# Two small tiles move to the right end of SBUF, and the pools of that side shift by 448 bytes

## The chip, the core and the metric

The kernel runs on one core of a Trainium2 chip. The metric is the device time of one execution in microseconds (us); the time of a kernel is the median of its runs. The core has a matrix engine (PE in the profile; PEld is its loading of weights), a vector engine (DVE), a scalar engine (ACT), GpSimd (POOL) and SyncE (SP), which here issues nearly all DMAs. Work is held in SBUF, 128 partitions; an address below is a byte offset within each partition.

## The reference

A trunk of two layers is applied to two groups of tokens, 512 and 256, of width 1,024, in float32 with shared weights. Cut to what matters:

```python
def swiglu(h, wg, wu, wd):
    return (jax.nn.silu(h @ wg) * (h @ wu)) @ wd

def even_layer(x, ...):                     # layer 0
    x = x + 0.5 * swiglu(rmsnorm(x, f1_n), f1_g, f1_u, f1_d)
    x = x + mixer_ab(rmsnorm(x, mix_n), ...)  # gMLP gating and windowed attention
    x = x + 0.5 * swiglu(rmsnorm(x, f2_n), f2_g, f2_u, f2_d)
    return x
# odd_layer (layer 1) is the same with mixer_c, a 2-D neighbourhood attention
# trunk: even_layer, odd_layer, final rmsnorm
```

The hidden width of the feed-forward blocks is 2,816. `rmsnorm(x, g)` multiplies by a scale vector `g`; there are seven of them, one for each of the six blocks and the final one.

## The kernel before

**Stages.** `build` (line 1408) runs six phases in order: `l0f1`, `l0m`, `l0f2`, `l1f1`, `l1m`, `l1f2`, that is, feed-forward, mixer, feed-forward for each layer, and then the final norm. The activations `x` stay in SBUF as 8 tiles of 128 features x 768 tokens, in two halves of 384 tokens.

**A product in float32.** Each operand is split into a high and a low part of type fp32r (`split`, line 193, for activations; `wsplit`, line 103, for weights: ACT copies the high part, DVE subtracts to get the low one). `mm3` (line 175) then issues three matmuls into one PSUM tile: high x high, high x low, low x high. All go through `mmul`, so they have line 139 in the profile. The first operand, weights, is loaded into the array; the second, the *moving* operand, streams through it.

**A feed-forward block.** `ffn` (line 416) works on 11 pairs of hidden tiles (`pair`, line 459), for `gate` and `up`. The product of a pair, 2 x 2 blocks in features, hidden units and tokens, is formed with seven block products in place of eight, from sums and differences of blocks. The combinations of the activations are made once per block: `b11`, `b21`, `t1`, `t2`, `t3`, `n4`, `b22`, each as four tiles of 128 x 384 for the high (`h`) and the low part (`l`). They live in the pool `comb` (`ffn_open`, `ffn_tiles`, lines 303 to 313). The sums of weights (`s`) and everything else of a pair live in the pool `work`: 30 buffers of 128 x 384 for hidden values and their split combinations (`db..`, `dt..`, `dn..`), and 8 of 128 x 512. A block product is 4 steps of 128 features x 3 matmuls of 384 columns. The first four pairs (`EARLY`) are interleaved, as their operands and the norm's scales come one after another. After every second pair `down` (line 628) multiplies the hidden values of two pairs by the down weights, again with seven products; the last two pairs go through `down_last` (line 693).

**Weights.** `raw` (line 91) issues a 512 KB DMA on SP's queue for each block of weights into a rotating pool of four buffers. The parts that `wsplit` makes, `whi` and `wlo`, rotate through five buffers each of the pool `w`.

**Order of the work.** The matmuls are issued in the order in which the program text writes them, with attention and norm steps woven in by a clock of estimated matmul time (`spawn`, `tick`). On the other engines the framework orders instructions by priority and by when their operands are there, and puts in every wait.

**Where tiles lie.** The pools made in `__init__` are allocated at the left end and stay: constants (`const`: identity, ones, the scale vectors `gains` and their negatives `ngains`), `x`, `raw`, `w`, `norm`. What is left between them and the right end of SBUF is shared by the pools of the phases, opened with a side (`open`, line 80), left or right, from which they grow. `comb` and `work` have opposite sides, and so have the mixer's pools `xg` (the split activations, later the split attention output) and `mp` (all else):

| Phase | left | right |
|---|---|---|
| `l0f1` | `work` | `comb` |
| `l0m` | `mp` | `xg` |
| `l0f2`, `l1f1` | `comb` | `work` |
| `l1m` | `xg` | `mp` |
| `l1f2` | `work` | `comb` |

In the built program the left ones begin at address 73,760 and the right ones end at 229,344. Pools are opened with `reuse_waits="tile"`: a tile in memory that an earlier pool has released waits for the last uses of the earlier tiles that it overlaps, not for the whole pool.

Of the kernel before, what the change touches and what calls it, by code (L numbers as in the profile page):

```python
# [9 lines left out]
F32 = mybir.dt.float32  # L10
# [6 lines left out]
P = 128  # L17
D = 1024
KD = D // P
# [9 lines left out]
NORMS = ("l0_ffn1_norm", "l0_mix_norm", "l0_ffn2_norm", "l1_ffn1_norm", "l1_mix_norm", "l1_ffn2_norm", "final_norm")  # L29
# [22 lines left out]
class Trunk:  # L52
# [4 lines left out]
    def __init__(self, ctx, tc, aps, phases=PHASES):  # L57
        self.tc, self.nc, self.aps, self.phases = tc, tc.nc, aps, phases
        self.units = []
        self.woff = self.pi = 0  # L60
        self.t = 0.0
        self.chains = []
        self.spare = []
        self.first = []
        self.copied = []
        pool = lambda name, bufs, **kw: ctx.enter_context(tc.tile_pool(name=name, bufs=bufs, **kw))
        self.cp = pool("const", 1)
        self.xp = pool("x", 1)
        self.rawp = pool("raw", 4)
        self.wp = pool("w", NW)  # L70
        self.np_ = pool("norm", 1)
        self.mm = pool("mm", 4, space=bass.MemoryType.PSUM)
        self.aux = pool("aux", 4, space=bass.MemoryType.PSUM)
        self.dram = pool("spill", 1, space=bass.MemoryType.DRAM)
        self.guards = {}
        self.side = "left"
# [1331 lines left out]
    def build(self):  # L1408
        nc = self.nc
        self.ident = self.cp.tile([P, P], F32, tag="ident", name="ident")  # L1410
        make_identity(nc, self.ident)
        self.ones = self.cp.tile([P, P], F32, tag="ones", name="ones")
        nc.gpsimd.memset(self.ones, 1.0)
        self.onesr = self.cp.tile([P, P], F32R, tag="onesr", name="onesr")
        nc.vector.tensor_copy(self.onesr, self.ones)
        self.gains = self.cp.tile([P, KD * len(NORMS)], F32, tag="gains", name="gains")
        nc.scalar.dma_start(self.gains, self.aps["gains"])
        self.ngains = self.cp.tile([P, KD * len(NORMS)], F32, tag="ngains", name="ngains")
        nc.gpsimd.tensor_scalar(out=self.ngains, in0=self.gains, scalar1=-1.0, scalar2=None, op0=ALU.mult)
        self.x = [self.xp.tile([P, T], F32, tag=f"x{m}", name=f"x{m}") for m in range(KD)]  # L1420
        todo = [KIND[p] for p in self.phases] + [("last", 6)]
        kind = todo[0][0]
        if kind == "f":
            self.ffn_open("right")
            self.ffn_tiles()
            self.fw = self.open("work", "left")
        elif kind != "last":
            self.mixer_tiles("right")
        self.norm_begin(todo[0])
        for h, (c0, c1) in enumerate(HALVES):  # L1430
            for m in range(KD):
                nc.sync.dma_start(self.x[m][:, c0:c1], self.aps["x"][m, :, c0:c1])
                if not (h and kind == "f"):
                    self.final(m, c0, c1)
                if h == 0 and m % 4 == 3 and kind == "f":
                    pre = f"{self.phases[0][:2]}_ffn{self.phases[0][3]}"
                    self.first += [self.raw(f"{pre}_w_{n}", 0, KD, m // 4 * 2 * P, P) for n in ("gate", "up")]
            if h and kind == "f":
                self.spawn(self.second())
            elif kind in ("f", "last"):  # L1440
                self.half_done(h)
            if kind == "last":
                self.drain()
        for i, ph in enumerate(self.phases):
            self.following = todo[i + 1]
            if i == 0 and "l1m" in self.phases:
                self.bias_tables()
            if ph == "l1m":
                while self.spare:
                    self.spare.pop(0)()  # L1450
            if ph == "l0m":
                self.mixer0()
            elif ph == "l1m":
                self.mixer1()
            else:
                self.ffn(f"{ph[:2]}_ffn{ph[3]}")
        self.drain()
        for n in list(self.guards)[::-1]:
            self.close(n)
# [103 lines left out]
```

## Time and profile before

| | |
|---|---|
| median of 3 runs | 2648.54 us |
| the runs | 2646.51, 2648.54, 2650.86 us |
| the profiled execution, first to last instruction | 2646.8 us |
| PE, PEld busy | 2576.9 us (97%), 2505.0 us (95%) |
| DVE, ACT, POOL busy | 2272.7 us (86%), 1369.5 us (52%), 87.9 us (3%) |
| mean granted clock of PE | 0.990 |
| moved by DMA | 218.99 MB, 83 GB/s |

The profile is one execution; it gives its span and no other time of that execution. Busy time is the union of an engine's instructions. Matmuls are pipelined: the duration of one (some 340 ns) is longer than the distance from one to the next, so the pace is read from how many fit in a stretch, or from the chain of waits. That chain is followed back from the last instruction, at each step to what released it or to the instruction before it on its engine; a piece of it in the listing is a run of instructions of one kind, with start, length and count. A row of a window gives, for each engine, busy us and the number of instructions, then the granted clock and the DMA's share and rate.

### The profile page before, as it was taken

What the parts mean: (1) busy time and instruction counts of PE and PEld (TensorE: products, weight loads), DVE (VectorE), ACT (ScalarE), POOL (GpSimd) and SP (SyncE); (2) the same over time, 40 slices, a digit from 0 to 9 for tenths busy, and PEclk for the clock granted to TensorE, in tenths of its full rate; (3) what the DMA queues carried; (4) which work ended last, traced back from release to release, by engine and by line L of the source; (5) the groups of instructions that cost most, each with busy time, mean ns of one, the idle gap of its engine ahead of it and who ended that gap; (6) DMA issues with size and microseconds to landing.
All of it is one profiled execution on the core that took longest, in us unless ns stands there. A gap on an engine that the chain in (4) does not pass through costs nothing.

```text
span 2646.8 us, 41176 instructions
## 1 busy us (share of the span) xinstructions
PE 2576.9 (97%) x15094; PEld 2505.0 (95%) x15094; DVE 2272.7 (86%) x4793; ACT 1369.5 (52%) x2851; POOL 87.9 (3%) x172
## 2 busy tenths in 40 slices
PE   7999999998999999999999999999999999999997
PEld 7999999987899999999999999989898999999997
DVE  8998889889769988898999888886677699988886
ACT  7544444555656544445654544454455465454443
POOL 0000000000100000000000000002222100000000
PEclk9999999999999999999999999999999999999999
DMA  5323222431222222222222221232221332222221
GB/s 173 127 83 91 76 79 66 133 98 37 86 74 100 80 80 65 80 72 88 96 80 80 64 80 65 84 119 65 63 63 40 104 104 80 80 72 72 70 83 56
DMA packets 83898, 218.99 MB, mean 83 GB/s; under 512 B 20080, under 2 KB 32880, under 8 KB 83696
## 3 DMA queue, kind: packets, MB, share of 16 engines
q1 hardware_dynamic: 83552, 216.34, 25.4%
q8 instruction: 118, 1.93, 0.3%
q14 instruction: 84, 0.69, 0.1%
q10 hardware_dynamic: 144, 0.03, 0.0%
HBM read 206.90 MB, written 15.07 MB: 84 GB/s over the span
## 4 chain that ended last, share of the span: by engine, by line
PE 88%; DVE 7%; ACT 2%; DMA 1%; issue 1%; SPq 0%; DVEq 0%; ACTq 0%
PE ps_mm L139 55%; PE ps_aux L139 32%; DVE wlo L114 1%; DMA raw<-in_w 1%; PE ps_aux L143 1%; ACT p L910 1%; DVE xl L738 1%; ACT whi L113 0%; DVE p L919 0%; DVE tl L196 0%; DVE p L904 0%; DVE s L608 0%; ACT xh L737 0%; DVE ol L196 0%; DVE x L705 0%
## 5 line engine op out<-in xcount | busy, mean ns | idle before, releaser
L113 ACT CAST whi<-s 128x512 fp32r<-128x512 f32 x496 | 305.4, 622 | 396.3 <-DVE s L608 142.8
L113 ACT CAST whi<-raw 128x512 fp32r<-128x512 f32 x512 | 312.3, 621 | 265.6 <-PE ps_mm L139 119.5
L114 DVE TENSOR_TENSOR wlo<-s,whi 128x512 fp32r<-128x512 f32 x496 | 338.3, 688 | 71.0 <-ACT whi L113 70.6
L114 DVE TENSOR_TENSOR wlo<-raw,whi 128x512 fp32r<-128x512 f32 x494 | 339.5, 695 | 26.7 <-ACT whi L113 23.8
L139 PE MATMUL ps_aux<-dt,whi 128*128 128x384 f32 x864 | 222.7, 339 | 2.1 <-ACT whi L113 2.1
L139 PE MATMUL ps_mm<-db,whi 128*128 128x384 f32 x864 | 221.6, 338 | 0.0
L139 PEld LDWEIGHTS ps_aux<-dt,whi 128*128 128x128 f32 x864 | 157.6, 189 | 2.4 <-ACT whi L113 2.4
L139 PEld LDWEIGHTS ps_mm<-db,whi 128*128 128x128 f32 x864 | 156.8, 188 | 0.0
L139 PE MATMUL ps_mm<-xh,whi 128*128 128x512 f32 (+1 forms) x416 | 147.5, 355 | 4.0 <-ACT xh L737 4.0
L139 PE MATMUL ps_aux<-dt,wlo 128*128 128x384 f32 x432 | 146.7, 340 | 0.2 <-DVE wlo L114 0.2
L139 PE MATMUL ps_mm<-db,wlo 128*128 128x384 f32 x432 | 146.1, 338 | 0.0
L139 PE MATMUL ps_mm<-xl,whi 128*128 128x512 f32 (+1 forms) x416 | 142.5, 343 | 1.1 <-DVE xl L738 1.1
L139 PE MATMUL ps_mm<-xh,wlo 128*128 128x512 f32 (+1 forms) x416 | 142.2, 342 | 0.0
L498 DVE TENSOR_TENSOR u<-ps_aux,u 128x384 f32<-128x384 f32 x176 | 97.6, 555 | 4.2 <-PE ps_aux L139 3.5
L608 DVE TENSOR_TENSOR s<-raw,raw 128x512 f32<-128x512 f32 x124 | 83.9, 688 | 18.1 <-DMA raw<-in_w 18.1
L139 PE MATMUL ps_aux<-dh,whi 128*128 128x384 f32 x384 | 98.4, 338 | 0.7 <-DVE x L705 0.7
L608 DVE TENSOR_TENSOR s<-raw 128x512 f32<-128x512 f32 x124 | 85.4, 690 | 14.2 <-DMA raw<-in_w 13.7
L910 ACT ACTIVATE p<-p,st 128x256 f32<-128x256 f32 (+3 forms) x144 | 69.1, 483 | 54.8 <-DVE st L908 54.6
L660 DVE TENSOR_TENSOR x<-ps_aux,x 128x384 f32<-128x384 f32 x160 | 86.6, 554 | 11.8 <-PE ps_aux L139 11.8
L493 ACT COPY u<-ps_mm 128x384 f32<-128x384 f32 x176 | 83.7, 476 | 24.6 <-PE ps_mm L139 24.5
L139 PE MATMUL ps_mm<-oh,whi 128*128 128x384 f32 x256 | 89.2, 348 | 4.6 <-DVE x L887 4.0
L139 PEld LDWEIGHTS ps_mm<-xh,whi 128*128 128x128 f32 x416 | 79.4, 191 | 14.6 <-ACT xh L737 4.9
(486 smaller groups left out, 8092.4 us busy)
## 6 DMA issues: line engine op xcount, KB each, us to landing
raw<-in_w SPq DMA_DIRECT2D x350, 512.0 KB, 3.6
xdm<-x SPq DMA_DIRECT2D x16, 384.0 KB, 2.3
x<-in_x SPq DMA_DIRECT2D x16, 192.0 KB, 5.7
x<-xdm SPq DMA_DIRECT2D x8, 384.0 KB, 3.3
xold<-xdm SPq DMA_DIRECT2D x8, 384.0 KB, 3.0
out_y<-y SPq DMA_DIRECT2D x8, 384.0 KB, 2.5
tab<-skew SPq DMA_DIRECT2D x8, 256.0 KB, 5.0
raw<-in_w SPq DMA_DIRECT2D x8, 256.0 KB, 2.6
```

The costliest lines, as they stand in the source:

```text
L113: nc.scalar.copy(hi, src)
L114: (eng or nc.gpsimd).tensor_tensor(out=lo, in0=src, in1=hi.bitcast(F32), op=ALU.subtract)
L139: self.nc.tensor.matmul(out, lhsT=lhsT, rhs=rhs, start=start, stop=stop, **kw)
L143: self.nc.tensor.transpose(out, src, self.ident)
L493: nc.scalar.copy(e[n, out], bank[key, n])
L498: nc.vector.tensor_tensor(out=t, in0=bank[key, n], in1=t, op=ALU.add)
L608: f = lambda o, x, y, op: self.nc.vector.tensor_tensor(out=o, in0=x, in1=y, op=op)
L660: nc.vector.tensor_tensor(out=o, in0=ps, in1=o, op=ALU.add)
L738: nc.vector.scalar_tensor_tensor(out=lo, in0=src, scalar=gain, in1=hi.bitcast(F32), op0=ALU.mult, op1=ALU.subtract)
L910: nc.scalar.activation(outs[i], outs[i], AF.Exp, bias=nm[:, i : i + 1], accum_out=sm[:, i : i + 1])
```

## The change

A pool `end` with one buffer per tile is opened on the right before all others of that side. `gains` and `ngains`, 128 x 56 float32 each (224 bytes per partition), are allocated there and no longer in `const`. In `const` a tile `space` of 448 bytes, which nothing writes or reads, takes their place, so that all that follows on the left keeps its address. All pools on the right end 448 bytes lower: at 228,896.

```diff
         self.np_ = pool("norm", 1)
+        self.endp = pool("end", 1, side="right")
         self.mm = pool("mm", 4, space=bass.MemoryType.PSUM)
...
-        self.gains = self.cp.tile([P, KD * len(NORMS)], F32, tag="gains", name="gains")
+        self.gains, self.ngains = (
+            self.endp.tile([P, KD * len(NORMS)], F32, tag=n, name=n) for n in ("gains", "ngains")
+        )
+        self.cp.tile([P, 112], F32, tag="space", name="space")
         nc.scalar.dma_start(self.gains, self.aps["gains"])
-        self.ngains = self.cp.tile([P, KD * len(NORMS)], F32, tag="ngains", name="ngains")
         nc.gpsimd.tensor_scalar(out=self.ngains, in0=self.gains, scalar1=-1.0, scalar2=None, op0=ALU.mult)
```

## The prediction

> **What bounds the kernel now.** I read the page first, for the engine that fills the span and for the chain that ended last.
>
> ```profile
> span 2646.8 us, 41176 instructions
> PE 2576.9 (97%) x15094; PEld 2505.0 (95%) x15094; DVE 2272.7 (86%) x4793; ACT 1369.5 (52%) x2851; POOL 87.9 (3%) x172
> PE 88%; DVE 7%; ACT 2%; DMA 1%; issue 1%; SPq 0%; DVEq 0%; ACTq 0%
> ```
>
> TensorE is busy in 97% of the span and holds 88% of the chain. A change that adds and removes no arithmetic can move the time by the pace at which matmuls follow each other, or by waits. So the second view is a table of four equal stretches, one from the steady part of each feed-forward block. Each holds the same work by the code: two pairs at 7 products x 2 names x 12 matmuls (336) and one `down` of two pairs, 7 x 2 x 4 x 3 (168), 504 matmuls of 384 columns. (The table counts matmuls that straddle an edge as well.)
>
> ```profile
> core 0: us, PE busy (x) PEld busy (x) DVE busy (x) ACT busy (x) POOL busy (x), PEclk, DMA share, GB/s
> 309.30:397.78 88.48, 88.48 (x506) 88.48 (x505) 77.54 (x140) 42.33 (x85) 0.00 (x0) 1.00 0.23 72
> 1064.68:1152.60 87.92, 87.92 (x505) 87.92 (x505) 77.34 (x141) 42.34 (x85) 0.00 (x0) 1.00 0.24 73
> 1557.90:1645.83 87.93, 87.93 (x506) 87.93 (x505) 77.50 (x141) 42.48 (x85) 0.00 (x0) 1.00 0.22 73
> 2414.67:2503.15 88.48, 88.48 (x505) 88.48 (x505) 77.48 (x140) 42.33 (x85) 0.00 (x0) 1.00 0.22 72
> ```
>
> PE is busy without a gap in all four, at the full granted clock, and yet the first and last take 0.56 us longer. The same program, with one thing different: in the first and last feed-forward block the operand tiles of the pairs (`comb`) are on the right and the hidden tiles for `down` (`work`) on the left; in the two in the middle it is the other way round. The chain of waits, piece by piece (start, length, what), shows where the 0.56 us are. First block, then second:
>
> ```profile
> 309.30 21.20 PE ps_mm L139 x120
> 330.50 8.48 PE ps_aux L139 x48
> 343.22 4.16 PE ps_aux L139 x24
> 347.39 8.32 PE ps_mm L139 x48
> 372.35 16.96 PE ps_mm L139 x96
> ```
>
> ```profile
> 1064.68 20.80 PE ps_mm L139 x120
> 1085.48 8.32 PE ps_aux L139 x48
> 1097.96 4.24 PE ps_aux L139 x24
> 1102.20 8.48 PE ps_mm L139 x48
> 1127.63 16.64 PE ps_mm L139 x96
> ```
>
> Rows 1, 2 and 5 are pairs, rows 3 and 4 are `down`. With the moving operand on the right a matmul takes 21.20/120 = 176.67 ns, on the left 20.80/120 = 173.33 ns; in `down` the sides have changed and so have the paces (8.32/48 = 173.33 and 8.48/48 = 176.67). The four stretches give the same two numbers on their own: 336r + 168l = 88.48 and 168r + 336l = 87.92 have r = 176.67, l = 173.33. So a moving operand on the right costs 3.33 ns more per matmul, 1.9%.
>
> The addresses of the built program say what differs. Left pools that are opened and closed begin at byte 73,760 of each partition, the right ones end at 229,344, and their 1,536-byte tiles keep the offset within 512 bytes: 32 on the left, 480 on the right. The region is not it: left `comb` reaches to 159,776, past 143,328 where right `comb` begins. The weights (`whi`, `wlo`) stay at offset 64.
>
> **The change, part by part.**
>
> *The move of the right pools.* 480 - 448 = 32: tiles on the right get the offset that the left ones have today. I take the pace of the left for them, because it is the pace of the same matmuls with the same weights at that very offset. It touches every moving operand on the right: 1,848 matmuls of pairs in each of the first and last block, 756 of `down` and 192 of the last `down` in each of the two middle ones, 384 of the first mixer's output projection; together 3,696 + 1,896 + 384 = 5,976. Not all of them are slow today:
>
> ```profile
> 81.03 12.72 PE ps_mm L139 x72
> 93.75 10.57 PE ps_aux L139 x60
> 153.36 12.58 PE ps_aux L139 x72
> 191.13 16.96 PE ps_mm L139 x96
> 460.83 21.20 PE ps_mm L139 x120
> 743.23 26.54 PE ps_mm L139 x153
> 2191.43 12.72 PE ps_mm L139 x72
> 2204.15 10.57 PE ps_aux L139 x60
> 2263.30 12.49 PE ps_aux L139 x72
> 2300.75 16.96 PE ps_mm L139 x96
> 2566.19 21.12 PE ps_mm L139 x120
> ```
>
> From 191 us on in the first block and from 2,300 in the last, all are slow (first and last piece of each: 176.67, 176.67, 176.67, 176.0): pairs 4 to 10, 2 x 7 x 168 = 2,352. Of the early pairs the pieces at 81, 94, 2,191 and 2,204 us are slow: 264. The `down` of pairs 0 to 8 in the middle blocks, as at 1,102 us: 2 x 756 = 1,512. That makes 4,128 x 3.33 ns = 13.8 us, the low end. Of the other 1,848 the 384 of the output projection are fast already (26.54/153 = 173.5), and the early pairs are fast in places (12.58/72 = 174.7, 12.49/72 = 173.5). Their excess, 1.4, 0.1 and 0.1 ns, is 40%, 4% and 4% of 3.33, so I count a fifth of 1,464 as slow: 290. **4,420 x 3.33 ns = 14.7 us.** The high end counts all but the output projection: 5,592 x 3.33 = 18.6 us. The mixers' other matmuls with an operand on the right have no equal on the left; 624 in the first mixer at 3.33 ns would be 2.1 us either way, and I take nothing, as the nearest row (743.23) runs fast there.
>
> *What PE's gain meets.* PE arrives earlier at waits that it does not set itself.
>
> ```profile
> PE ps_mm L139 <- ACT whi L113: 12.8, 4, 8.3
> 253.13 0.78 PE L139 MATMUL ps_aux<-dt,whi 128*128 128x384 f32 x2 [2.12 <-ACT whi L113]
> 253.00:257.00 4.00, 3.71 (x12) 0.57 0.00 0
> ```
>
> In the steady stretches there is none: DVE needs 77.5 of 87.9 us, so at 87.4 it is at 89%, and at 87.92 PE lost no time to it. In the early pairs there is, as at 253 us. Ahead of it stand about 360 slow matmuls of the first block (1.2 us), ahead of the last such wait of the last block about 270 (0.9 us). If ACT is not moved by PE there, these 2.1 us are given back; if it waits for buffers that PE frees, none. I take 1.0. The wait also brought a half granted clock (0.57 over 4 us), which costs 4 x 0.43 = 1.7 us; one such drop more or less is in the range, not in the sum.
>
> *The vectors, and the `space` tile.* The DMA of `gains` and the negation on GpSimd are the same instructions to other addresses, once, in the first 20 us; nothing. DVE and ACT read and write tiles of the right at the same speed; here `s`, on the left in the first stretch and on the right in the second:
>
> ```profile
> L114 DVE TENSOR_TENSOR wlo<-s,whi 128x512 fp32r<-128x512 f32 x24 | 16.4, 691 | 4.9 <-ACT whi L113 4.8
> L113 ACT CAST whi<-s 128x512 fp32r<-128x512 f32 x25 | 15.3, 621 | 23.5 <-PE ps_mm L139 6.8 <-PE ps_aux L139 6.4 <-issue 6.0
> ...
> L114 DVE TENSOR_TENSOR wlo<-s,whi 128x512 fp32r<-128x512 f32 x24 | 16.3, 688 | 4.9 <-ACT whi L113 4.9
> L113 ACT CAST whi<-s 128x512 fp32r<-128x512 f32 x25 | 15.3, 621 | 22.6 <-PE ps_mm L139 6.3 <-PE ps_aux L139 6.2 <-issue 5.9
> ```
>
> The `space` tile fills the 448 bytes left free, is never used, and keeps `x` and all left pools where they are: nothing.
>
> *Waits on reused memory.* A tile waits for released tiles that it overlaps. Between tiles of the same side nothing shifts; between sides, by 448 bytes, the neighbour met may be another. The pairs that come closest in time are the second mixer's (right) over the old `comb` (left):
>
> ```profile
> L139 PE MATMUL ps_mm<-t33h,wlo x22: 336/336/339, 1320.7 to 1725.1; 128*128 128x384 f32 x22
> L1190 SPq DMA_DIRECT2D bb<-tab x4: 319/372/431, 1781.6 to 1794.7; - x4
> ```
>
> The last reader is done 56 us before the first writer; a neighbour's last read (all of `comb` within a few us) changes none of that. Nothing on SP's queue or any other is moved. I set zero.
>
> Sum: 2,646.8 - 14.7 + 1.0 = 2,633.1 us for the profiled execution. Its span is 1.7 us under the median of the runs, 2,648.54; from the median, **2,634.8 us**.
>
> A rule speaks against all this. The Trainium skill, "TensorE: Matmul & The Clock Gate", section "Step-by-step: what each phase is for", says that the array reads the moving operand and the weights through two independent ports, so that loading weights takes nothing from a running matmul; by it a tile's place costs nothing and the time would stay at 2,648.5 us. The trace does not agree: 176.67 against 173.33 ns for equal work.
>
> **The rivals.** *No change.* The slow pace may belong to something other than the offset within 512 bytes: to which pools were opened at the right end, or to what PE read just before. For it: stretches on the right that run fast (743.23, 2263.30), so the offset does not make a matmul slow by itself. Against: no steady piece on the left is slow. Time: 2,648.5. The skill's rule of the two ports would give this one too.
>
> *Half of it.* After the move, pairs on the right have high parts at offset 544 within 1,024 bytes and low parts at 32, where the left `comb` has them the other way round (today 992 and 480). If only one arrangement is fast, pairs stay slow and `down` gains: 1,512 x 3.33 = 5.0 us, 2,643.5.
>
> *Slower.* Today the sides have different offsets. If the fast pace needed the two to differ, and a common offset 32 put both into the slow one, the 5,976 matmuls of 384 columns on the left would lose 3.33 ns and the right would stay: +19.9 us, 2,668.4. It decides from the point where more matmuls run slow than today's 4,420. For it: no row shows both sides at one offset. Against: the left piece keeps 173.33 beside right pieces and among left ones.
>
> **How the numbers follow.** Forecast 0.80, half 0.06, no change 0.08, slower 0.06. About 0.2% (5.3 us) is what a measurement here can tell from no change. The half case at 2,643.5 is on the edge and counts half as faster, half as same: faster 0.83, same 0.11, slower 0.06. The forecast's own range: 18.6 us and a half-clock drop less (1.7) give 2,628.2; 13.8 less 2.1 and a drop more (1.7) give 2,638.5. To hold 8 in 10 with a part of the half case the range is 2,628 to 2,643.
>
> **What would show it.** All four stretches should read near 504 x 173.33 = 87.36 us; the pieces of 120 should be 20.80 and those of 96 16.64 in all blocks; PE's busy time should fall by about 14 us, with PE's waits for ACT and DVE up by 1 us or so and all DVE and ACT rows as they are. Wrong if right pieces keep 21.20, if left ones rise, or if the gain appears in the stretches but waits between blocks grow by as much.

## The result, and the profile after

| | before | after |
|---|---|---|
| median of 5 runs each, us | 2648.76 | 2637.14 |
| the runs, us | 2646.51 to 2650.86 | 2633.24 to 2638.39 |
| the profiled execution's span, us | 2646.8 | 2631.1 |

The ratio is 0.9953, with a 95% interval of 0.9941 to 0.9965: the kernel became 9.3 to 15.6 us faster. The forecast was 2634.8 us, 13.7 below the median of before; the medians measured here are 11.6 us apart.

The page of the changed kernel, in the three lines that stand first in the prediction (lines of code that were 139 before are 140 now):

```profile
span 2631.1 us, 41175 instructions
PE 2560.5 (97%) x15094; PEld 2487.4 (95%) x15094; DVE 2268.0 (86%) x4793; ACT 1365.8 (52%) x2851; POOL 87.7 (3%) x172
PE 88%; DVE 8%; ACT 2%; DMA 1%; issue 1%; SPq 0%; DVEq 0%; ACTq 0%
```

Every engine runs the same instructions, and TensorE, VectorE and ScalarE run them in the same order, but for two neighbouring matmuls of the first mixer that changed places. (The total is one lower: one semaphore instruction of SP is gone.) TensorE is busy 16.4 us less for the same 15,094 matmuls. The table of four stretches, with the same work in each as before:

```profile
core 0: us, PE busy (x) PEld busy (x) DVE busy (x) ACT busy (x) POOL busy (x), PEclk, DMA share, GB/s
307.37:394.73 87.36, 87.36 (x505) 87.36 (x505) 77.29 (x141) 42.23 (x85) 0.00 (x0) 1.00 0.24 73
1056.13:1143.49 87.36, 87.36 (x506) 87.36 (x505) 77.34 (x141) 42.32 (x85) 0.00 (x0) 1.00 0.24 73
1546.84:1634.20 87.36, 87.36 (x506) 87.36 (x505) 77.31 (x141) 42.33 (x85) 0.00 (x0) 1.00 0.25 73
2401.11:2488.47 87.36, 87.36 (x505) 87.36 (x505) 77.12 (x141) 42.21 (x85) 0.00 (x0) 1.00 0.24 73
```

All four last 504 x 173.33 ns = 87.36 us: the blocks no longer differ, and both sides have the pace that the left had. The chain of waits of the changed kernel shows the pieces (start, length, what); the first three are early pairs, the fourth and the next to last the first steady pairs of their block, the sixth a `down`. The third holds two short waits, so its 12.75 us for 72 matmuls are not a pace:

```profile
80.64 12.48 PE ps_mm L140 x72
93.12 10.40 PE ps_aux L140 x60
152.54 12.75 PE ps_aux L140 x72
190.48 16.64 PE ps_mm L140 x96
307.37 20.80 PE ps_mm L140 x120
344.81 8.32 PE ps_mm L140 x48
739.14 26.55 PE ps_mm L140 x153
2288.79 16.64 PE ps_mm L140 x96
2550.87 20.80 PE ps_mm L140 x120
```

21.20 became 20.80, 16.96 became 16.64, and the output projection (26.55, it was 26.54) stayed. The waits of TensorE that grew most (engine and line, what it waited for, total, times, longest):

```profile
PE ps_mm L140 <- ACT whi L114: 13.3, 5, 8.6
PE ps_aux L140 <- DVE x L706: 1.4, 2, 0.7
```

They were 12.8 us, 4 times, and 0.7 us, once: 1.2 us more. Other waits became shorter: in all, TensorE idled 2,631.1 - 2,560.5 = 70.6 us of the span, against 2,646.8 - 2,576.9 = 69.9 before, 0.7 us more.

Where did the 15.7 us between the two profiled executions go? Cut at the same instructions, the spans fall into three kinds of stretches. In the last column the pace is taken from the start-to-start times of the 384-column matmuls in the two traces (those of 160 to 200 ns, that is, without waits and half clock): the difference of the means times the number.

```
stretches                                     before    after     gain   of it pace
steady parts of the four blocks              1146.58  1136.25    10.33         10.8
beginnings of the blocks, early pairs          809.26   803.17     6.09          3.6
the two mixers, the end                        690.96   691.68    -0.72          0.5
sum                                           2646.80  2631.10    15.70         14.9
```

So the pace is worth 14.9 us. The early part of the second block gives more than its pace, and its windows say why; first before, then after, around the same work:

```profile
743.00:780.00 37.00, 34.98 (x193) 34.30 (x191) 22.15 (x45) 16.64 (x33) 3.87 (x3) 0.95 0.20 64
880.00:900.00 20.00, 19.87 (x102) 19.27 (x103) 18.44 (x35) 10.57 (x21) 0.00 (x0) 0.91 0.29 106
```

```profile
739.00:776.00 37.00, 34.99 (x202) 34.35 (x201) 23.04 (x48) 17.65 (x34) 3.88 (x3) 1.00 0.21 64
876.00:896.00 20.00, 19.87 (x115) 19.58 (x114) 19.68 (x38) 10.67 (x22) 0.00 (x0) 1.00 0.27 86
```

Two drops of the granted clock behind waits, 37 x 0.05 + 20 x 0.09 = 3.7 us, are in the profiled execution of before and not in that of after. They come and go between executions of one kernel (the next experiment's profiled execution has both again), so the medians, 11.6 us apart, are the better measure of the change, and the 15.7 us contain some luck. It is not all one way: two other stretches at half clock, from 1,769 and 2,618 us, last 13.7 and 15.0 us after, where they lasted 10.2 and 13.7 us before. That fits the mixers and the end, which became slower. Over the whole span 54.5 us at half clock became 52.5, which is worth 1.0 us.

### The profile page after: what moved, and what is told of

Same layout as the page of the kernel before. It is cut to its first block, busy times and chain, and to the rows that moved or that the text cites. A ratio compares the mean times of both kernels' runs of the same rounds, so it can differ in the third digit from the quotient of the medians.

```text
span 2631.1 us, 41175 instructions
## 1 busy us (share of the span) xinstructions
PE 2560.5 (97%) x15094; PEld 2487.4 (95%) x15094; DVE 2268.0 (86%) x4793; ACT 1365.8 (52%) x2851; POOL 87.7 (3%) x172
## 4 chain that ended last, share of the span: by engine, by line
PE 88%; DVE 8%; ACT 2%; DMA 1%; issue 1%; SPq 0%; DVEq 0%; ACTq 0%
PE ps_mm L140 55%; PE ps_aux L140 32%; DVE wlo L115 1%; PE ps_aux L144 1%; DMA raw<-in_w 1%; ACT p L911 1%; DVE xl L739 1%; DVE p L905 1%; DVE p L920 0%; DVE tl L197 0%; ACT whi L114 0%; ACT xh L738 0%; DVE s L609 0%; DVE ol L197 0%; DVE x L706 0%
## 5 line engine op out<-in xcount | busy, mean ns | idle before, releaser
L140 PEld LDWEIGHTS ps_mm<-xh,whi 128*128 128x128 f32 x416 | 79.5, 191 | 14.7 <-ACT xh L738 4.9
```

The lines of the kernel that those rows point to most:

```text
L140: self.nc.tensor.matmul(out, lhsT=lhsT, rhs=rhs, start=start, stop=stop, **kw)
```

## The experiments

The prediction named one cause, the offset of the moving operand within 512 bytes, and it was read from two offsets, 32 and 480, beside weights that always lay at 64. Four things differ together there, and the first group of runs takes them apart. Theory A: the moving operand's own offset, 480, is slow. Theory B: it is the distance from the moving operand to the weights in the array, which went from 416 (480 - 64) to -32 (32 - 64), modulo 512. Theory C: what is slow is the use of two offsets side by side, and one common offset is fast. Beside them: it is the vectors' own place, or the distance from the end of SBUF.

All kernels below start from the kernel before and add only unused tiles, so the vectors stay in `const`, and all instructions keep their order. A pad on the right lowers the right pools, a pad on the left raises the left ones, and one between `raw` and `w` raises the weights and all left pools behind them.

**pad448: the shift without the move of the vectors.**

```diff
         self.np_ = pool("norm", 1)
+        self.rpad = pool("rpad", 1, side="right")
+        self.rpad.tile([P, 112], F32, tag="rpad", name="rpad")
```

> The vectors stay in const; an unused tile of 448 bytes in a pool at the right end shifts the right pools alone (moving operands on the right at offset 32 within 512 bytes, weights at 64, left at 32). Offset theory, in all its forms: all right matmuls of 384 columns at 173.33 ns, steady stretches of 87.36 us, median 2637 us, as with the whole change. Rival, that the vectors' new place or the emptied place in const brought the gain: pace 176.67 ns on the right as before and 2649 us.

Measured: 2635.14 us (2632.76 to 2639.66), ratio 0.9944 (0.9932 to 0.9956). The chain, a steady piece of the first block and one of the last:

```profile
308.04 20.80 PE ps_mm L141 x120
2495.21 20.80 PE ps_mm L141 x120
```

The shift alone brings the whole gain; where the vectors lie adds nothing that can be measured. The profiled execution, which has the two clock drops, at 772 and 878 us, again, was the slowest of the five.

**pad512: the same with 512 bytes**, so that the right keeps offset 480.

```diff
+        self.rpad = pool("rpad", 1, side="right")
+        self.rpad.tile([P, 128], F32, tag="rpad", name="rpad")
```

> As the 448-byte shift, but by 512 bytes: the right pools lie lower and end clear of the right end, yet keep offset 480 within 512 bytes. Offset theory with a period of 512: nothing changes, 176.67 ns on the right, stretches of 88.48 and 87.92 us, 2649 us. Rival, that any distance from the right end or from the old neighbours will do (reuse of memory, the end itself): 173.33 ns on the right and about 2637 us.

Measured: 2647.92 us, ratio 0.9992 (0.9984 to 1.0001). First and second block:

```profile
309.58 21.20 PE ps_mm L141 x120
1062.12 20.80 PE ps_mm L141 x120
```

All is as before the change. So it isn't the distance from the end of SBUF, nor which tile of the other side lies next: a shift by 512 bytes changes nothing that can be measured.

**wshift448: the weights move, the two sides come to a common 480.** The pad raises the weights to offset 0 and the left pools to 480; the right ones stay at 480. Both sides are then at distance -32.

```diff
         self.rawp = pool("raw", 4)
+        self.wpad = pool("wpad", 1)
+        self.wpad.tile([P, 112], F32, tag="wpad", name="wpad")
```

> An unused tile of 448 bytes ahead of the weight pool: the weights go from offset 64 to 0 and the left pools from 32 to 480; the right pools stay at 480. Theory A, the moving operand's own offset decides (480 slow): now both sides are slow, stretches near 504 x 176.67 ns = 89.04 us, some 14 to 18 us more than before, about 2664 us. Theory B, the distance from the moving operand to the weights decides (-32 fast, as left before; -96 slow, as right before): both sides are at -32 now, stretches of 87.36 us, about 2637 us. Theory C, the two sides must have one offset: 2637 us too.

Measured: 2636.65 us, ratio 0.9946 (0.9934 to 0.9958).

```profile
308.72 20.80 PE ps_mm L141 x120
1057.36 20.80 PE ps_mm L141 x120
```

Every moving operand is at 480, and every piece is fast. Theory A, the prediction's, falls. B and C both stand.

**left448: both sides at 480, the weights at 64**, so that the offsets are common and the distance is 416 on both sides.

```diff
         self.np_ = pool("norm", 1)
+        self.lpad = pool("lpad", 1)
+        self.lpad.tile([P, 112], F32, tag="lpad", name="lpad")
```

> An unused tile of 448 bytes behind the weight pool and the norm's pool: only the left pools shift, to offset 480; right pools at 480 and weights at 64 stay. Theories A (own offset) and B (distance to the weights): both sides slow, stretches near 89.04 us, about 2664 us. Theory C (the two sides must have one offset): both fast, 87.36 us, about 2637 us.

Measured: 2643.15 us (12 runs, 2639.30 to 2651.74), ratio 0.9977 (0.9967 to 0.9988). Steady pieces of the first two blocks, and early ones of the second and third:

```profile
309.05 20.80 PE ps_mm L141 x120
838.18 12.72 PE ps_mm L141 x72
1061.72 20.80 PE ps_mm L141 x120
1332.13 12.72 PE ps_mm L141 x72
```

Neither theory has it. The steady parts are fast at the distance that was slow before, against B; some early pairs, those from 824 to 876 us for one, run at 12.72/72 = 176.67 ns, against C. The start-to-start times of consecutive matmuls show where such a stretch begins (start of the run in us, moving operand and its offset, then ns):

```
left448    819.99  t3   at 480   ... 173 173 174 173 174
           823.88  diag at  64   178 170
           824.23  t3   at 480   176 179 174 179 174 179
           825.29  n4   at 480   174 180 174 179 174 179 174 180 174 179 ...
after      817.14  t3   at  32   ... 173 174 173 173 174
           821.04  diag at  64   176 171
           821.39  t3   at  32   171 176 177 178 175 174
           822.44  n4   at  32   175 173 174 173 173 174 173 173 174 173 ...
```

There are two steady rhythms, 173-173-174 and 174-179, and the same tiles at the same distance run in the one or in the other. What changes it is two matmuls by which the norm spreads its scales: their moving operand `diag`, a tile of the pool `norm`, lies at 64. Behind them left448 stays in the slow rhythm until TensorE has to wait (at 877 us), and the changed kernel is back in the fast one after some eight matmuls. The step from one side to the other does the same in before: at 283.70 us, where the pairs on the right follow the `down` on the left, 173-174 turns into 174-179 within three matmuls.

From this comes theory D: a jump of the moving operand's offset can start the slow rhythm, and the distance to the weights decides whether it then stays until a wait or until a tile at another distance (416), or dies out (-32).

The second group tries D against the rivals that the right side itself is slow, or that only a step in one direction is.

**mirror: the two offsets change sides.** Left 480, right 32, weights at 64.

```diff
+        self.lpad = pool("lpad", 1)
+        self.lpad.tile([P, 112], F32, tag="lpad", name="lpad")
+        self.rpad = pool("rpad", 1, side="right")
+        self.rpad.tile([P, 112], F32, tag="rpad", name="rpad")
```

> Unused tiles of 448 bytes behind the norm's pool on the left and at the right end: left pools at offset 480, right pools at 32, weights at 64, the two sides exchanged against the kernel before. Theory D (a jump of the moving operand's offset starts the slow pace; at distance -96 from the weights it stays until a wait or a tile at another distance, at -32 it dies out within some six matmuls): left matmuls slow at 176.67 ns, right ones fast at 173.33; the four stretches read 87.92, 88.48, 88.48 and 87.92 us; about 2649 us, as before. Rival (the right side itself is the slow one when the sides differ): right slow as before, stretches 88.48, 87.92, 87.92, 88.48. Rival (the slow side is the one entered by a forward jump): 480 to 32 is a forward jump, so again the right would be slow.

Measured: 2652.05 us, ratio 1.0014 (1.0006 to 1.0023). First block: a pair, then a `down`; second block: the same.

```profile
308.34 20.80 PE ps_mm L143 x120
354.34 8.48 PE ps_aux L143 x48
1064.77 21.20 PE ps_mm L143 x120
1111.17 8.32 PE ps_aux L143 x48
```

The sides have exchanged their paces, pairs and `down` alike. The right side is not slow by itself, and the slow stretches now follow the step from the right to the left. In offsets this is still the step from 32 to 480, as in before; that it is not this step as such is shown by w0 below, where the step from 480 to 32 leads into the slow stretches.

**nojump480: left448 without the jump.** Pads bring the tiles of `norm`, `diag` among them, to offset 480 too, and move `onesr`, the operand in the array while `diag` streams, from 128 to 64; the left pools are at 480 as in left448.

```diff
         self.wp = pool("w", 5)
+        self.dpad = pool("dpad", 1)
+        self.dpad.tile([P, 104], F32, tag="dpad", name="dpad")
         self.np_ = pool("norm", 1)
+        self.lpad = pool("lpad", 1)
+        self.lpad.tile([P, 8], F32, tag="lpad", name="lpad")
...
+        self.cp.tile([P, 112], F32, tag="space", name="space")
         self.onesr = self.cp.tile([P, P], F32R, tag="onesr", name="onesr")
+        self.cp.tile([P, 16], F32, tag="space2", name="space2")
```

> Like the shift of the left pools alone (both sides at 480, weights at 64, distance -96 everywhere), and in addition the diagonal tiles of the norm go to offset 480 and the ones they are multiplied with to 64, so that in the feed-forward blocks no moving operand of 384 columns and no weights change their offset. Theory D: nothing starts the slow pace any more, the stretches of it in the early pairs (68 to 123, 823 to 897, 2173 to 2227 us with the left shift alone) are gone, and the time goes from 2643 to about 2637 us. Rival (at distance -96 the waits of the early pairs start it): the stretches stay, 2643 us.

Measured: 2638.84 us, ratio 0.9971 (0.9959 to 0.9983) to a before of 2648.27 on that chip. The two early pieces, which were 12.72 in left448:

```profile
834.26 12.48 PE ps_mm L143 x72
1327.18 12.48 PE ps_mm L143 x72
```

The slow stretches of the early pairs behind `diag` are gone, though every moving operand is at the distance that is slow in before. So distance 416 is not slow by itself, and the jump of `diag` did start these stretches. (Both operands of the `diag` matmuls were moved at once, so this run does not say which of the two mattered there; at the step from side to side it is the moving operand alone that changes its offset.) The whole time doesn't show it: the intervals of this ratio and of left448's overlap.

But a jump isn't the only start. In this same trace the last pair of the second block falls into the slow rhythm behind a short wait, with no step of the offset anywhere near. The weight load of the first `n4` matmul waits 0.23 us:

```profile
1221.87 0.19 PEld L143 LDWEIGHTS ps_mm<-n40h,whi 128*128 128x128 f32 x1 [0.23 <-ACT u L497]
```

```
nojump480  1220.58  t3 at 480   173 174 173 173 174 173
           1221.62  t3, n4      251 290
           1222.16  n4 at 480   176 172 176 178 174 180 174 179 174 179 174 180 174 179 ...
```

It stays there for 70 matmuls, 176.6 ns each, to the end of the pair. The end of a half-clock stretch can do it too, as at 882 us in left448. Nor does every wait act so: behind the wait at 820 us, where two starts are 0.84 us apart, left448 runs in the fast rhythm. What is left of D is this: at distance 416 a jump, and sometimes a short wait or a change of clock, starts the slow rhythm, which then stays, as a rule until a wait or a tile at another distance (in before it ends once without either, at 2,583 us). Where nothing starts it, the fast one stays.

**s64 and s256: other distances, with a jump between the sides.** s64 moves both sides inward by 64 bytes (left 96, right 416: distances 32 and 352), s256 by 256 (left 288, right 224: 224 and 160).

```diff
+        self.lpad = pool("lpad", 1)
+        self.lpad.tile([P, 16], F32, tag="lpad", name="lpad")     # s256: 64
+        self.rpad = pool("rpad", 1, side="right")
+        self.rpad.tile([P, 16], F32, tag="rpad", name="rpad")     # s256: 64
```

> Left pools up by 64 and right pools down by 64: left at offset 96 (distance +32 from the weights), right at 416 (distance -160). What the distance does is known for -32 (fast) and -96 (slow after a jump) alone. If the slow pace belongs to a narrow band of distances, both sides run at 173.33 ns; if to all distances but a narrow band around -32, both are slow and stretches read 89.0 us.

> Left pools up by 256 and right pools down by 256: left at offset 288 (distance +224), right at 224 (distance +160). As for the smaller shift: both at 173.33 ns if the slow distances are a narrow band, both slow if the fast ones are.

Measured: s64 2666.50 us (one run), s256 2650.46 (one run). s64, a pair of the first block and two pieces of the second, ahead of its third `down` and behind it:

```profile
311.46 21.20 PE ps_mm L143 x120
982.73 20.80 PE ps_mm L143 x120
1071.13 21.20 PE ps_mm L143 x120
```

Both sides are slow for the most part, and that costs 18 us over before; as these kernels ran once, the pieces say more than the times. The second row is an exception: left tiles at distance 32 run at 173.33 ns from 958 to 1,016 us, although the `down` just before used the right, and at 176.67 from 1,045 us on; the third block has the same change between 1,513 and 1,543 us. So at this distance either rhythm can stay, and a jump doesn't start the slow one every time. In s256 the left is fast and the right slow, as before the change:

```profile
307.60 21.20 PE ps_mm L143 x120
1059.75 20.80 PE ps_mm L143 x120
```

**s32 and l224r352: four more distances.** s32 has pads of 32 bytes (left 64, right 448: distances 0 and 384), l224r352 of 224 and 352 (left 256, right 128: 192 and 64).

```diff
+        self.lpad = pool("lpad", 1)
+        self.lpad.tile([P, 8], F32, tag="lpad", name="lpad")      # l224r352: 56
+        self.rpad = pool("rpad", 1, side="right")
+        self.rpad.tile([P, 8], F32, tag="rpad", name="rpad")      # l224r352: 88
```

> Left pools up by 32, right pools down by 32: left at offset 64 (distance 0 from the weights), right at 448 (distance -128). Seen so far: distances -32 and +224 recover after a jump; -96, -160, +32 and +160 keep the slow pace. Theory D with a period of 256 bytes in the distance (-32 and 224 are one residue, -96 and 160 another) says nothing of 0 and 128; with the fast ones a narrow band around -32 both sides are slow, stretches of 89.0 us and about 2665 us; with a band that reaches to 0 the left is fast, stretches of 88.5 and 87.9 us as before.

> Left pools up by 224 (offset 256, distance 192), right pools down by 352 (offset 128, distance 64). The last two residues of 256 in steps of 32. Narrow band around 224: both slow, about 2665 us. A band from 192 to 224: left fast, right slow, about 2649 us.

Measured: s32 2656.37 us, l224r352 2644.35 (one run each; before 2651.16 on that chip). Right and left of each, in the first and second block:

```profile
310.71 21.12 PE ps_mm L143 x120
1066.06 20.80 PE ps_mm L143 x120
```

```profile
310.35 20.80 PE ps_mm L143 x120
1059.67 20.96 PE ps_mm L143 x120
```

s32: 176.0 ns on the right, 173.33 on the left. l224r352: 173.33 on the right, and on the left 174.67, a third level.

**w0: the moving operands as before, the weights elsewhere.** The weights go from 64 to 0, and a second pad brings the left pools back to 32: for the pairs and `down` only the distances change, to 32 on the left and 480, that is -32, on the right.

```diff
         self.rawp = pool("raw", 4)
+        self.wpad = pool("wpad", 1)
+        self.wpad.tile([P, 112], F32, tag="wpad", name="wpad")
...
         self.np_ = pool("norm", 1)
+        self.lpad = pool("lpad", 1)
+        self.lpad.tile([P, 16], F32, tag="lpad", name="lpad")
```

> Weights at offset 0 in place of 64 (an unused tile of 448 bytes ahead of their pool), a second one of 64 behind the norm's pool; so the moving operands keep the very offsets of before, 32 on the left and 480 on the right. Theory D, by the distance to the weights: left at +32 slow, right at -32 fast, the sides exchanged: stretches 87.92, 88.48, 88.48, 87.92 us, about 2650 us. Rival, that the moving operand's own offset decides: right slow as before, stretches 88.48, 87.92, 87.92, 88.48 us.

Measured: 2651.62 us, ratio 1.0002 (0.9992 to 1.0013).

```profile
308.83 20.80 PE ps_mm L143 x120
1065.30 21.20 PE ps_mm L143 x120
```

The offsets 32 and 480 are those of before, and the paces have changed sides: 480 is fast and 32 is slow. This is the cleanest separation of all: what decides is not the moving operand's own offset but where it lies from the weights.

Together, where the two sides differ, the mean pace in the steady parts (start-to-start times of 160 to 200 ns, from the 49th matmul of pair 4 on) by the distance modulo 512:

```
distance      0     32     64    160    192    224    352    384    416    480
pace, ns  173.3   slow  173.3  176.6  174.8  173.4  176.7  176.0  176.6  173.4
(32: 175.9 in s64, where some stretches are fast, and 176.7 in w0; 416: 176.5 to 176.7, three kernels)
```

160 and 416 agree, and so do 224 and 480: the period may be 256 rather than 512, which two pairs suggest and don't prove. No distance is faster than 173.33 ns, so nothing here points to a kernel that beats the changed one.

## Why the prediction was right, and where its reason was not

*The pace.* The step "tiles on the right get the offset that the left ones have today", with its 3.33 ns per matmul, held: 20.80, 16.64 and 87.36 us came as told. The term of 14.7 us for 4,420 slow matmuls measured 14.9 us. Of it 2 x (1,128 + 504) x 3.33 ns = 10.9 us lay in the steady parts (pairs on the right in the outer blocks, `down` in the middle ones), where 10.8 us were found; the other 3.8 us, with the guess of a fifth of the early matmuls in it, met 3.6 in the early parts and 0.5 in the mixers and the end.

*Its cause.* "480 - 448 = 32" gave the right number from an incomplete cause. The offset within 512 bytes is not what counts (wshift448, w0), but the distance to the weights, together with the jumps and short waits that start the slow rhythm. The prediction could not see it, as the weights lay at 64 throughout and the offset and the distance were the same quantity; and moving the right side to 32 removed the bad distance and the jump between the sides at once. That the number came out rests on this: the change gave the right side the distance of the left, and not only its offset. By the same step the prediction would have taken wshift448 and left448, with both sides at 480, for slow kernels, and w0 for one with its sides as before. The objection that it raised itself, fast stretches on the right, fits the missing half: the slow rhythm needs a start.

*The give-back.* "I take 1.0" between 0 and 2.1; TensorE's idle time grew by 0.7 us, but the closeness is luck. The waits that the prediction named did not grow: the one at 253 us (in a `down`, not in the early pairs) was 2.12 us and still is, and the one at 2,231 us in the last block was 1.50 and still is. The first of before stands in the prediction; the other of before, then both of after:

```profile
2230.82 0.44 PE L139 MATMUL ps_mm<-t20h,whi 128*128 128x384 f32 x1 [1.50 <-ACT whi L113]
251.36 0.62 PE L140 MATMUL ps_aux<-dt,whi 128*128 128x384 f32 x2 [2.12 <-ACT whi L114]
2219.00 0.44 PE L140 MATMUL ps_mm<-t20h,whi 128*128 128x384 f32 x1 [1.50 <-ACT whi L114]
```

So nothing was given back there, as in the prediction's other case, in which ACT waits for buffers that PE frees. What grew lies elsewhere, 0.2 us of it in the kernel's first wait. The half-clock drops, put at 1.7 us each way, were the larger uncertainty: two are missing in the profiled execution of after, and the runs of that kernel spread over 5 us.

*What was set to zero.* The vectors and the `space` tile (pad448), DVE and ACT, and the waits on reused memory: nothing of these showed. The `s` casts read 620 ns, 622 before:

```profile
L114 ACT CAST whi<-s 128x512 fp32r<-128x512 f32 x496 | 304.6, 620 | 390.3 <-DVE s L609 149.4 <-PE ps_mm L140 116.9 <-issue 74.6
```

*The rivals.* No change, and with it the reading that a tile's place costs nothing, falls with the pieces. Half of it falls as well: pairs on the right are fast with their parts the other way round within 1,024 bytes. The slower case had the sign of a true thing reversed: the two sides' offsets do matter to each other, but it is their being equal that is fast in the steady parts (after, wshift448, left448), and their differing that mostly lets the slow rhythm begin. Its price was near that of another layout by chance: s64, with both sides slow, took 2666.5 us against its 2668.4.

## What to carry to other kernels

Where TensorE is busy without a gap and two stretches of equal work differ by a per cent or two, compare the addresses of the moving and the stationary operands: a few hundred unused bytes can be worth 0.5% here, and others cost 0.7%. The safest layout found is one in which all moving operands of a stretch have the same distance to the weights, and that distance is one at which the rhythm recovers (-32 here). And before a cause is named from one contrast, list what else has the same contrast: here the offset and the distance went together throughout the trace, and only moving the weights could part them.

## What the runs showed of the hardware that was not expected

A stream of 384-column fp32r matmuls at the full granted clock, each with a weight load beside it, has more than one steady rhythm: 173-173-174 ns, 174-179 ns, and levels between (174.67, 176.0). Which one it is depends on the distance in SBUF between the two operands and on what ran before: left448 and nojump480 have the same operands at the same distance, 12.72 and 12.48 us for the same 72 matmuls. The Trainium skill, "SBUF — State Buffer", section "SBUF: two separate sides", says that TensorE never waits on another engine's access. Nothing here contradicts that, as it is TensorE's own two operands whose places matter to each other: in w0, of the operands of the pairs and `down`, the weights alone moved, and the paces of the sides, 173.33 and 176.67 ns, changed places.

What stays open: the mechanism inside. That the two reads meet in the memory is a guess that fits the distances; no record shows a pause as such. Nor is it known how a jump starts the slow rhythm, why some short waits start it and others end it, and why it stays at these distances and not at others.
